# Low parts of the split weights computed on VectorE alone, in a two-block fp32 kernel on one Trainium2 core

## The chip, the cores and the metric

The program runs on one core of a Trainium2 chip. The metric is the device time of one execution in microseconds (us). One execution was also taken by the hardware profiler, and every row below comes from that one. The engines are PE (TensorE, the matrix products), DVE (VectorE), ACT (ScalarE), POOL (GpSimd) and SP (SyncE, which issues the DMAs).

## The reference

All is fp32, for 256 tokens of width 1024 (and 256 tokens of context in the first layer). A first block has two layers whose norms are scaled, shifted and gated by rows of an "ada" projection; a second block has two layers with layer norms after each step.

```python
# first block, for each of two layers
m_lat = silu(c) @ ada_w[l] + ada_b[l]           # shifts, scales, gates
h = rmsnorm(x, norm_g[l, 0]) * (1 + sc1) + sh1
y = pool_hgrn_mixer(...) if l % 2 == 0 else gqa_mixer(...)
x = x + g1 * rmsnorm(y, norm_g[l, 1])
f = swiglu(rmsnorm(x, norm_g[l, 2]) * (1 + sc2) + sh2, ffn_w_in[l], ffn_w_out[l])
x = x + g2 * rmsnorm(f, norm_g[l, 3])
...
# second block, for each of two layers
swiglu_2 = lambda x, wg, wu, wd: (silu(x @ wg) * (x @ wu)) @ wd
# x = layer_norm(alpha * x + 0.5 * swiglu_2(x))          first half step
# x = layer_norm(alpha * x + mixer(x))                   attention + RG-LRU, or delta rule
# x = layer_norm(alpha * x + 0.5 * swiglu_2(x))          second half step
# x = x + sigmoid(x @ wg + bg) * (p @ wp)                a gated embedding
```

## The kernel before

**Products.** A product of fp32 matrices is made of three products of rounded parts. A weight tile that has come by DMA (`raw`) is split by `split` (L149): ACT copies it to a rounded high part `hi` (L151), and another engine subtracts to give the low part, `lo = raw - hi` (L152). Activations are split by the same function into `xh` and `xl`, or `hh` and `hl`. `mm3` (L174, products on L176) adds hi·xh, lo·xh and hi·xl in PSUM. PSUM has tiles of four kinds, `A` (three), `B` (two), `tr` (two, for transposes) and `C` (one).

**Weights.** `piece` (L154) brings 128 x 2048 numbers of a weight by two DMAs on SP's queue (L163) into two of four `raw` tiles, and splits each in two quarters of 128 x 512: four quarters, so four ACT copies and four subtractions, for a piece. A `raw` tile is free for the next DMA when both of its quarters are split. In the second block four pieces of `hi` and `lo` are in turn.

**Where a low part is made.** `split` takes a flag: with it the subtraction goes to POOL (`self.G`), else to DVE (`self.V`). `piece` sets that flag for the second quarter of each `raw` tile when the attribute `spread` is true. `spread` is true in three places: for the first unit's weights of each feed-forward part that has one stream (`ffn`, L362; five such parts: `f1` of the first block's second layer, and `f00`, `f02`, `f10`, `f12` of the second block), through `ab2_mixer` (the second block's first mixer), and through `delta_mixer` (its second), the big projections of both among it. In all 66 subtractions go to POOL.

**Order.** Each engine works through its instructions in the order in which the build puts them. DVE's list holds the subtractions between the steps of norms and mixers; POOL's holds its subtractions between the powers (L270) that give a norm its inverse root.

**The joints between two parts.** At the end of a step of the second block `finish` in `post_ln` does, for each of the two token tiles: L1048 (add the product from PSUM), L1049 and L1053 (statistics), L275 (DVE, `rv`), L270 (POOL, `pow`), L1056 and L1058 (normalise; two halves each), then `to_xT` transposes on PE (L239, tiles `tr`) and splits. The next part's products can't start for that token tile before. In the first block the same is done by L697 (add), L662 with L270 (root), L655 (scale, tile `big`) and L239; in the gated embedding by L1094 to L1097. In `delta_mixer` a small weight `wraw` (columns 4096 to 4111) is split by `split` too, and its products (L1290) run among the first projection's; each of 24 blocks of 128 features of the projections is then evacuated by `conv`: three steps L1348 and one L1351 on DVE. In between go the 16 steps of a logarithm (L322, L324) and the products and decays of the delta rule (L1388, L1389, L1402).

**Gates.** `ada_gate` makes a gate row by a product with one column of the identity matrix; the change leaves it.

Of the kernel before, what the change touches and what calls it, by code (L numbers as in the profile page):

```python
# [9 lines left out]
F32 = mybir.dt.float32  # L10
# [3 lines left out]
ALU = mybir.AluOpType  # L14
# [67 lines left out]
class Kern:  # L82
# [40 lines left out]
    def buffers(self, es, raw, split):  # L123

        self.w = self.pool("w", 1, es, reuse_waits="tile")
        self.nraw, self.nsplit = raw, split
# [17 lines left out]
        self.tc.cur_priority -= n  # L144


    spread = False

    def split(self, hi, lo, src, pool=False):  # L149

        self.S.activation(hi, src, AF.Copy)  # L151
        (self.G if pool else self.V).tensor_tensor(lo, src, hi.bitcast(F32), op=ALU.subtract)  # L152

    def piece(self, shape, srcs, perm=None):  # L154

        hi = self.t(self.w, shape, "hi", F32R, bufs=self.nsplit)
        lo = self.t(self.w, shape, "lo", F32R, bufs=self.nsplit)
        m = shape[1] // 2
        n = shape[-1] // 2
        for h in range(2):  # L160
            raw = self.t(self.w, [shape[0], m, *shape[2:]], "raw", bufs=2 * self.nraw)
            for dst, src in srcs(raw):
                self.dma(dst, src[:, h * m:(h + 1) * m])  # L163
            for i in range(2):
                if m % 2:
                    a, b = (slice(None), h, slice(i * n, i * n + n)), (slice(None), 0, slice(i * n, i * n + n))
                else:
                    a, b = (slice(None), slice((2 * h + i) * m // 2, (2 * h + i + 1) * m // 2)), (slice(None), slice(i * m // 2, (i + 1) * m // 2))
                self.split(hi[a], lo[a], raw[b], i == 1 and self.spread)
        return hi, lo  # L170

    aside = iter(())
# [167 lines left out]
    def ffn(self, xT, streams, gate, up, down, splits, hpool, finish, ypool=None, each=None):  # L340

        gv, uv = (w.rearrange("(k p) f -> p k f", p=P) for w in (gate, up))
        dv = down.rearrange("(k p) f -> p k f", p=P)
        nS = len(streams)
        tiles = [2 * s + j for s in streams for j in range(2)]
        acc = {}
        u0 = 0
        for r, nu in enumerate(splits):  # L350
            hs, first = [], []
            for u in range(nu):
                c0 = (u0 + u) * 256
                h = [self.t(hpool, [P, nS, 2, 256], n, F32R, bufs=max(splits) + (len(splits) > 1)) for n in ("hh", "hl")]
                hs.append(h)
                if nS == 2:
                    pcs = [self.piece([P, 4, 2, 256], lambda t, k=k: [
                        (t[:, :, 0], gv[:, 4 * k:4 * k + 4, c0:c0 + 256]),
                        (t[:, :, 1], uv[:, 4 * k:4 * k + 4, c0:c0 + 256])]) for k in range(2)]
                    self.up_both(pcs, h, hpool, r == u == 0, each)  # L360
                    continue
                self.spread = u < 1  # L362
                pcs = [self.piece([P, 8, 256], lambda t, wv=wv: [(t, wv[:, :, c0:c0 + 256])]) for wv in (gv, uv)]
                self.spread = False

                if u < 2:
                    first.append((pcs, h))
                    if u:
                        for tl in tiles:
                            for pcs, h in first:  # L370
                                self.up_tile(xT[0], tl, pcs, h, hpool)
                else:
                    self.up_one(xT[0], pcs, h, hpool)
            nk = 2 * nu
            last = r == len(splits) - 1

            def hT(tl, kc):
                c = slice((tl % 2) * P, (tl % 2) * P + P)
                return [x[:, streams.index(tl // 2), kc % 2, c] for x in hs[kc // 2]]

            def out(tl, half, ps, r=r, last=last):
                if len(splits) == 1:
                    return finish(tl, half, ps, None)
                if r == 0:
                    acc[tl, half] = self.t(ypool, [P, 512], f"y{tl}_{half}")
                    self.S.activation(acc[tl, half], ps, AF.Copy)
                else:
                    self.V.tensor_add(acc[tl, half], acc[tl, half], ps)
                if last:
                    finish(tl, half, None, acc[tl, half])  # L390

            self.down(hT, tiles[2:] + tiles[:2] if last else tiles, dv[:, 2 * u0:2 * u0 + nk], nk, out)
            u0 += nu
# [730 lines left out]
    def ab2_mixer(self, xT):  # L1124
        d, V, S, G, T = self.d, self.V, self.S, self.G, self.T
        w = d["ab_w_in_2"][0]
        with self.scope("a2") as hp:
            cw, cb, ba, bx_, rate, nrate = self.rg
            gate_w = []
            for nm in ("b_wa_2", "b_wx_2"):  # L1130
                m = self.t(hp, [P, 4, P], nm)
                G.memset(m, 0.0)
                src = d[nm][0].rearrange("(b two) i j -> two i b j", two=2)
# [29 lines left out]
            kT = self.t(hp, [P, 2, 256], "kT")  # L1163
            vv = {}

            self.spread = True
            def queries(t, ps):
                q = self.t(hp, [P, 512], "q")
                S.activation(q, ps, AF.Copy)
                pt = self.pst((P, 4, P))  # L1170
                self.transposes(pt, q, range(4))
                S.activation(qT[:, :, t * P:(t + 1) * P], pt, AF.Copy)
# [63 lines left out]
            a = self.t(hp, [P, 4, 256], "a")  # L1236
# [22 lines left out]
                V.tensor_tensor_scan(hs[:, b], a[:, b], ig[:, b], 0.0, ALU.mult, ALU.add)  # L1259
            V.scalar_tensor_tensor(hs, hs, 0.5, g2, op0=ALU.mult, op1=ALU.mult)  # L1260
            self.split(cat[0][:, 4:8], cat[1][:, 4:8], hs)
            self.spread = False
        return cat


    def delta_mixer(self, xT):
        d, V, S, G, T = self.d, self.V, self.S, self.G, self.T
        w = d["c_w_in_2"][0]
        with self.scope("dl") as hp:
# [7 lines left out]
            raw = self.t(hp, [P, 8, 16], "wraw")  # L1277
# [7 lines left out]
            def rates():  # L1285

                ps = self.ps((P, 256))
                for kc in range(8):
                    for i, (x, y) in enumerate(((0, 0), (1, 0), (0, 1))):
                        T.matmul(ps, wb[x][:, kc], xT[y][:, kc], start=kc + i == 0, stop=kc == 7 and i == 2)  # L1290
                        yield
                ba = self.t(hp, [16, 256], "ba")
                S.activation(ba, ps[0:16], AF.Copy)
                pt = self.pst((P, 2, 16))
                for t in range(2):
                    T.transpose(pt[:, t], ba[:, own[t]], self.ident[0:16, 0:16])
                    yield
                S.activation(beta, pt[:, :, 0:8], AF.Sigmoid)
                V.tensor_add(ad, pt[:, :, 8:16], dtb.unsqueeze(1).to_broadcast([P, 2, 8]))
                sp = self.softplus(both(ad), 16)  # L1300
                V.scalar_tensor_tensor(g, sp.rearrange("p (t h) -> p t h", t=2), -1.0, nea.unsqueeze(1).to_broadcast([P, 2, 8]),
                                       op0=ALU.mult, op1=ALU.mult)
# [251 lines left out]
                    self.split(oT[0][:, hs, own[t]], oT[1][:, hs, own[t]], pt)  # L1554

            all4 = [(hg, t) for hg in range(2) for t in range(2)]
            self.spread = True
            with self.among(rates()):
                gates(0)
            steps = lambda *its: (x for it in its for x in it)  # L1560
# [13 lines left out]
            inverse(all4)  # L1574
            for t in range(2):
                outputs(t, range(2))
            self.spread = False
        return oT


# [4 lines left out]
    def block1(self):  # L1585
# [3 lines left out]
        with contextlib.ExitStack() as es:  # L1589
# [30 lines left out]
            def products(g):  # L1620
                for h in range(2):
                    for k in (2 * g, 2 * g + 1):
                        self.mm3(q0[h], *(x[:, k, h * P:(h + 1) * P] for x in piece), self.xh[:, :, k], self.xl[:, :, k], k == 0, k == 7)
# [210 lines left out]
```

## Time and profile before

| | |
|---|---|
| device time, 3 runs | 2187.03 us median (2185.43 to 2190.0) |
| profiled execution | 2189.62 us, of which span 2187.8 us |
| granted TensorE clock, mean of the profiled execution | 0.989 of full speed |
| PE / DVE / ACT / POOL busy | 96% / 63% / 44% / 12% of the span |

How to read the rows further down: a row of a group has the line, the engine, the operation, what it writes and reads, the number of instructions, their busy time, and the mean time of one in ns; then the idle time before them and its releaser. A row of waits says which engine and line waited for which, how long in total, how many times, and the longest. A row of the windows has, for a stretch of the span, the busy time of each engine and the granted TensorE clock.

### The profile page before, as it was taken

What the parts mean: (1) busy time and instruction counts of PE and PEld (TensorE: products, weight loads), DVE (VectorE), ACT (ScalarE), POOL (GpSimd) and SP (SyncE); (2) the same over time, 40 slices, a digit from 0 to 9 for tenths busy, and PEclk for the clock granted to TensorE, in tenths of its full rate; (3) what the DMA queues carried; (4) which work ended last, traced back from release to release, by engine and by line L of the source; (5) the groups of instructions that cost most, each with busy time, mean ns of one, the idle gap of its engine ahead of it and who ended that gap; (6) DMA issues with size and microseconds to landing.
All of it is one profiled execution on the core that took longest, in us unless ns stands there. A gap on an engine that the chain in (4) does not pass through costs nothing. (4 is left out here: it accounts for less than half of the span.)

```text
span 2187.8 us, 34008 instructions
## 1 busy us (share of the span) xinstructions
PE 2103.7 (96%) x13178; PEld 1827.5 (84%) x13178; DVE 1368.1 (63%) x2430; ACT 970.0 (44%) x1904; POOL 255.0 (12%) x248
## 2 busy tenths in 40 slices
PE   7999999999999999999999889999999999999998
PEld 4787878788887668998998778998899788879987
DVE  4746658765536786555654677555755587876556
ACT  4332353322225456444544475444544355355443
POOL 0524210000000210001000401000100155120000
PEclk9999999999999999999999999999999999999999
DMA  9632427666431334565765527655665463136653
GB/s 310 231 101 78 135 75 232 222 220 203 126 115 49 132 97 153 177 190 156 220 189 184 169 79 216 187 183 167 204 185 183 153 162 111 49 120 208 184 183 105
DMA packets 238941, 352.58 MB, mean 161 GB/s; under 512 B 14432, under 2 KB 185020, under 8 KB 238652
## 3 DMA queue, kind: packets, MB, share of 16 engines
q1 hardware_dynamic: 238780, 350.41, 51.4%
q8 instruction: 104, 1.70, 0.3%
q14 instruction: 57, 0.47, 0.1%
HBM read 349.31 MB, written 1.05 MB: 160 GB/s over the span
## 5 line engine op out<-in xcount | busy, mean ns | idle before, releaser
L151 ACT ACTIVATE hi<-raw 128x512 fp32r<-128x512 f32 (+1 forms) x1072 | 601.4, 617 | 736.3 <-issue 367.8
L152 DVE TENSOR_TENSOR lo<-raw,hi 128x512 fp32r<-128x512 f32 x1006 | 670.7, 709 | 396.0 <-ACT hi L151 394.4
L176 PE MATMUL B<-xh,hi 128*128 128x256 f32 (+1 forms) x1200 | 366.6, 306 | 1.6 <-ACT r L1141 1.4
L176 PE MATMUL B<-xl,hi 128*128 128x256 f32 (+1 forms) x1200 | 366.0, 305 | 1.0 <-DVE xl L152 0.9
L176 PE MATMUL B<-xh,lo 128*128 128x256 f32 (+1 forms) x1200 | 366.0, 305 | 0.0
L176 PE MATMUL A<-xh,hi 128*128 128x256 f32 (+1 forms) x1008 | 304.5, 302 | 3.1 <-ACT a L1389 2.9
L176 PE MATMUL A<-xh,lo 128*128 128x256 f32 (+1 forms) x1008 | 303.2, 301 | 0.7 <-DVE lo L152 0.7
L176 PE MATMUL A<-xl,hi 128*128 128x256 f32 (+1 forms) x1008 | 303.3, 301 | 0.0
L176 PEld LDWEIGHTS B<-xh,hi 128*128 128x128 f32 x1200 | 229.2, 191 | 11.9 <-ACT r L1141 1.6
L176 PEld LDWEIGHTS B<-xl,hi 128*128 128x128 f32 x1200 | 229.3, 191 | 11.2 <-DVE xl L152 1.9
L176 PEld LDWEIGHTS B<-xh,lo 128*128 128x128 f32 x1200 | 229.1, 191 | 10.1 <-issue 1.2
L176 PEld LDWEIGHTS A<-xh,hi 128*128 128x128 f32 x1008 | 193.4, 192 | 11.7 <-ACT a L1389 3.1
L176 PEld LDWEIGHTS A<-xh,lo 128*128 128x128 f32 x1008 | 193.2, 192 | 7.9 <-DVE lo L152 1.5
L176 PEld LDWEIGHTS A<-xl,hi 128*128 128x128 f32 x1008 | 193.5, 192 | 6.1
L176 PE MATMUL B<-hi,xh 128*128 128x512 f32 (+1 forms) x464 | 171.4, 370 | 5.5 <-DVE r L1048 2.7
L176 PE MATMUL B<-lo,xh 128*128 128x512 f32 (+1 forms) x464 | 169.6, 366 | 0.0
L176 PE MATMUL B<-hi,xl 128*128 128x512 f32 (+1 forms) x464 | 169.0, 365 | 0.0
L270 POOL TENSOR_TENSOR pow<-rv,mhalf 128x1 f32<-128x1 f32 (+2 forms) x54 | 43.2, 801 | 994.8 <-DVE rv L275 509.2
L152 POOL TENSOR_TENSOR lo<-raw,hi 128x512 fp32r<-128x512 f32 x66 | 96.1, 1470 | 467.0 <-ACT hi L151 464.7
L176 PE MATMUL B<-hi,hl 128*128 128x512 f32 x308 | 122.1, 396 | 0.0
L176 PE MATMUL A<-hi,hl 128*128 128x512 f32 x308 | 121.9, 396 | 0.0
L176 PE MATMUL A<-hi,hh 128*128 128x512 f32 x308 | 121.8, 395 | 0.0
(439 smaller groups left out, 3429.1 us busy)
## 6 DMA issues: line engine op xcount, KB each, us to landing
adaw<-in_ada_w SPq DMA_DIRECT2D x96, 512.0 KB, 4.8
raw<-in_ffn_wg SPq DMA_DIRECT2D x88, 512.0 KB, 4.8
raw<-in_ffn_wu SPq DMA_DIRECT2D x88, 512.0 KB, 4.6
raw<-in_ffn_wd SPq DMA_DIRECT2D x88, 512.0 KB, 4.3
raw<-in_ffn_w_in SPq DMA_DIRECT2D x88, 256.0 KB, 4.4
raw<-in_ffn_w_in SPq DMA_DIRECT2D x44, 512.0 KB, 4.4
raw<-in_ab_w_in SPq DMA_DIRECT2D x38, 512.0 KB, 4.4
raw<-in_ffn_w_out SPq DMA_DIRECT2D x38, 512.0 KB, 4.3
```

The source lines that it names most:

```text
L151: self.S.activation(hi, src, AF.Copy)
L152: (self.G if pool else self.V).tensor_tensor(lo, src, hi.bitcast(F32), op=ALU.subtract)
L176: self.T.matmul(ps, l, r, start=first and i == 0, stop=last and i == 2)
L270: self.G.tensor_tensor(r, x, exponent_tile[:, :x.shape[1]], op=ALU.pow)
```

## The change

All 66 low parts that POOL made are made by DVE. `spread` and the flag of `split` go; nothing is computed differently. The rest of POOL's work (powers, elementwise steps of the mixers, memsets) stays on POOL.

```diff
-    spread = False
-
-    def split(self, hi, lo, src, pool=False):
+    def split(self, hi, lo, src):
 
         self.S.activation(hi, src, AF.Copy)
-        (self.G if pool else self.V).tensor_tensor(lo, src, hi.bitcast(F32), op=ALU.subtract)
+        self.V.tensor_tensor(lo, src, hi.bitcast(F32), op=ALU.subtract)
...
-                self.split(hi[a], lo[a], raw[b], i == 1 and self.spread)
+                self.split(hi[a], lo[a], raw[b])
...
-                self.spread = u < 1
                 pcs = [self.piece([P, 8, 256], lambda t, wv=wv: [(t, wv[:, :, c0:c0 + 256])]) for wv in (gv, uv)]
-                self.spread = False
...
-            self.spread = True
             def queries(t, ps):
...
-            self.spread = False
         return cat
...
-            self.spread = True
             with self.among(rates()):
...
-            self.spread = False
         return oT
```

The lines of the changed kernel are a few lower (L152 is L150, L1048 is L1044, L1058 is L1054, L1348 is L1342). The order on the engines moves too, since it is made anew. Three places on DVE follow; each row is one or two instructions (x2), with the tiles' own numbers.

First, where `f00`'s last norm meets `ab2_mixer`: `lo_11037`, `lo_11051` and `lo_11369` are weights of the mixer, `r_1499` is the second token tile. Before:

```order
L152 TENSOR_TENSOR lo_11051<-raw_11052,hi_11050 128x512
L152 TENSOR_TENSOR lo_11051<-raw_11058,hi_11050 128x512
L1048 SCALAR_TENSOR_TENSOR r_1499_9030<-B_10674,r_1499_9030 128x512
L1048 SCALAR_TENSOR_TENSOR r_1499_9030<-B_10675,r_1499_9030 128x512
L1049 BN_STATS bns_10969<-r_1499_9030 128x6 x2
L152 TENSOR_TENSOR lo_11369<-raw_11370,hi_11368 128x512
L1053 BN_AGGR bna_10974<-bns_10969 128x2
L152 TENSOR_TENSOR lo_11369<-raw_11376,hi_11368 128x512
L275 TENSOR_SCALAR rv_10976<-bna_10974 128x1
L1056 SCALAR_TENSOR_TENSOR r_1499_9030<-r_1499_9030,bna_10974,lng_9025 128x512 x2
L1058 SCALAR_TENSOR_TENSOR r_1499_9030<-r_1499_9030,pow_10978,lnb_9027 128x512 x2
```

And now:

```order
L150 TENSOR_TENSOR lo_11037<-raw_11044,hi_11036 128x512 x2
L1044 SCALAR_TENSOR_TENSOR r_1499_9030<-B_10674,r_1499_9030 128x512
L1044 SCALAR_TENSOR_TENSOR r_1499_9030<-B_10675,r_1499_9030 128x512
L1045 BN_STATS bns_10969<-r_1499_9030 128x6 x2
L150 TENSOR_TENSOR lo_11051<-raw_11052,hi_11050 128x512
L1049 BN_AGGR bna_10974<-bns_10969 128x2
L150 TENSOR_TENSOR lo_11051<-raw_11052,hi_11050 128x512
L273 TENSOR_SCALAR rv_10976<-bna_10974 128x1
L1052 SCALAR_TENSOR_TENSOR r_1499_9030<-r_1499_9030,bna_10974,lng_9025 128x512 x2
L1054 SCALAR_TENSOR_TENSOR r_1499_9030<-r_1499_9030,pow_10978,lnb_9027 128x512 x2
```

The two subtractions just ahead of the second tile's norm belong to one piece now, and stand where those of two pieces stood: as many subtractions are queued ahead of L1058, and the weights that come later are pushed behind it.

Second, the same joint between `ab2_mixer`'s output product and `f02`: `lo_12008`, `lo_12022` and `lo_12038` are `f02`'s weights. Before:

```order
L1049 BN_STATS bns_11964<-r_1841_11776 128x6 x2
L152 TENSOR_TENSOR lo_12022<-raw_12029,hi_12021 128x512
L1053 BN_AGGR bna_11969<-bns_11964 128x2
L152 TENSOR_TENSOR lo_12038<-raw_12039,hi_12037 128x512
L275 TENSOR_SCALAR rv_11971<-bna_11969 128x1
L1056 SCALAR_TENSOR_TENSOR r_1841_11776<-r_1841_11776,bna_11969,lng_11771 128x512 x2
L1058 SCALAR_TENSOR_TENSOR r_1841_11776<-r_1841_11776,pow_11973,lnb_11773 128x512 x2
L152 TENSOR_TENSOR lo_12038<-raw_12039,hi_12037 128x512
L152 TENSOR_TENSOR lo_12038<-raw_12045,hi_12037 128x512
L152 TENSOR_TENSOR xl_68<-tr_11979,xh_67 128x4x128
```

And now:

```order
L1045 BN_STATS bns_11964<-r_1841_11776 128x6 x2
L150 TENSOR_TENSOR lo_12008<-raw_12015,hi_12007 128x512
L1049 BN_AGGR bna_11969<-bns_11964 128x2
L150 TENSOR_TENSOR lo_12022<-raw_12023,hi_12021 128x512
L273 TENSOR_SCALAR rv_11971<-bna_11969 128x1
L1052 SCALAR_TENSOR_TENSOR r_1841_11776<-r_1841_11776,bna_11969,lng_11771 128x512 x2
L1054 SCALAR_TENSOR_TENSOR r_1841_11776<-r_1841_11776,pow_11973,lnb_11773 128x512 x2
L150 TENSOR_TENSOR lo_12022<-raw_12023,hi_12021 128x512
L150 TENSOR_TENSOR lo_12022<-raw_12029,hi_12021 128x512
L150 TENSOR_TENSOR xl_68<-tr_11979,xh_67 128x4x128
```

Here the weights are one piece later than they were: `lo_12022`, whose split was done before the transposes, is now split around them. On PE the transposes into `tr_11979` and `tr_11986` stand 15 and 16 rows earlier than before.

Third, the projections of `delta_mixer`, in the middle of the values' blocks (`v`). Before:

```order
L1348 SCALAR_TENSOR_TENSOR cy_17136<-B_17059,colsC_9012,cy_17136 128x255
L1351 SCALAR_TENSOR_TENSOR v_2473_17044<-v_2473_17044,cy_17136 128x256
L152 TENSOR_TENSOR lo_17473<-raw_17474,hi_17472 128x512
L1348 SCALAR_TENSOR_TENSOR cy_17182<-A_17143,colsC_9012,cy_17182 128x253
L1348 SCALAR_TENSOR_TENSOR cy_17182<-A_17143,colsC_9012,cy_17182 128x254
L152 TENSOR_TENSOR lo_17473<-raw_17480,hi_17472 128x512
L1348 SCALAR_TENSOR_TENSOR cy_17182<-A_17143,colsC_9012,cy_17182 128x255
```

And now:

```order
L1342 SCALAR_TENSOR_TENSOR cy_17136<-B_17059,colsC_9012,cy_17136 128x255
L150 TENSOR_TENSOR lo_17393<-raw_17400,hi_17392 128x512
L1345 SCALAR_TENSOR_TENSOR v_2473_17044<-v_2473_17044,cy_17136 128x256
L1496 TENSOR_TENSOR b2e_2570_17630<-b_2454_16890,egc_16175 128x4
L150 TENSOR_TENSOR lo_17473<-raw_17474,hi_17472 128x512
L1342 SCALAR_TENSOR_TENSOR cy_17182<-A_17143,colsC_9012,cy_17182 128x253
L150 TENSOR_TENSOR lo_17473<-raw_17474,hi_17472 128x512
L1342 SCALAR_TENSOR_TENSOR cy_17182<-A_17143,colsC_9012,cy_17182 128x254
L150 TENSOR_TENSOR lo_17473<-raw_17480,hi_17472 128x512
```

Twice as many subtractions stand between the steps that evacuate the blocks.

## Rows read from the trace of the kernel before

**Rows 1.** The page's busy times of the engines.

```profile
PE 2103.7 (96%) x13178; PEld 1827.5 (84%) x13178; DVE 1368.1 (63%) x2430; ACT 970.0 (44%) x1904; POOL 255.0 (12%) x248
```

**Rows 2.** Instructions of L152: count, then shortest/median/longest in ns.

```profile
L152 DVE TENSOR_TENSOR lo<-raw,hi x1006: 415/685/1812, 30.9 to 2169.3; 128x512 fp32r<-128x512 f32 x164, 128x256 fp32r<-128x256 f32 x4
...
L152 POOL TENSOR_TENSOR lo<-raw,hi x66: 1264/1356/1777, 812.2 to 1959.8; 128x512 fp32r<-128x512 f32 x66
```

**Rows 3.** Groups on DVE from 900 to 1000 us, without POOL subtractions.

```profile
L152 DVE TENSOR_TENSOR lo<-raw,hi 128x512 fp32r<-128x512 f32 x70 | 44.9, 687 | 35.2 <-ACT hi L151 35.2
```

**Rows 4.** Groups on DVE from 1215 to 1233 us, the start of `ab2_mixer`.

```profile
L152 DVE TENSOR_TENSOR lo<-raw,hi 128x512 fp32r<-128x512 f32 x6 | 7.5, 1279 | 0.0
L1058 DVE SCALAR_TENSOR_TENSOR r<-r,pow,lnb 128x512 f32<-128x512 f32 x4 | 3.8, 1001 | 0.0
```

**Rows 5.** Groups on POOL from 1215 to 1233 us.

```profile
L152 POOL TENSOR_TENSOR lo<-raw,hi 128x512 fp32r<-128x512 f32 x6 | 8.7, 1463 | 3.6 <-ACT hi L151 3.5
```

**Rows 6.** Timeline of DVE there: start us, duration us (of all of a row).

```profile
1224.35 1.28 DVE L1048 SCALAR_TENSOR_TENSOR r<-B,r 128x512 f32<-128x512 f32 x2
1225.55 1.27 DVE L1049 BATCH_NORM_STATS2 bns<-r 128x6 f32<-128x512 f32 x2
...
1230.43 1.40 DVE L1058 SCALAR_TENSOR_TENSOR r<-r,pow,lnb 128x512 f32<-128x512 f32 x2
```

**Rows 7.** Waits of PE from 1215 to 1236 us.

```profile
PE tr L239 <- DVE r L1058: 3.9, 2, 3.2
```

**Rows 8.** Windows: length; busy PE, PEld, DVE, ACT, POOL; clock; DMA share; GB/s.

```profile
1768.00:1870.00 102.00, 93.58 (x722) 89.52 (x721) 81.96 (x169) 55.70 (x117) 53.37 (x42) 0.97 0.46 126
1215.00:1236.00 21.00, 17.05 (x85) 14.48 (x84) 18.22 (x24) 9.82 (x18) 11.30 (x11) 0.92 0.63 199
1536.00:1558.00 22.00, 18.94 (x102) 16.45 (x101) 19.28 (x25) 14.68 (x26) 6.42 (x4) 0.92 0.76 235
1738.00:1768.00 30.00, 25.03 (x113) 19.38 (x112) 24.39 (x30) 14.08 (x28) 16.80 (x13) 0.89 0.56 155
1948.00:1970.00 22.00, 19.52 (x93) 16.12 (x93) 18.95 (x27) 13.36 (x24) 7.23 (x5) 0.92 0.60 180
```

**Rows 9.** Waits of SP's queue over the whole span.

```profile
SPq L163 <- POOL lo L152: 70.4, 43, 4.8
```

**Rows 10.** Waits of PE from 812 to 1035 us (`f1`, and where `f00` starts).

```profile
PE tr L239 <- DVE big L655: 2.8, 2, 2.2
PE tr L239 <- DVE r L697: 2.3, 2, 1.8
```

**Rows 11.** Instructions of L655: count, then shortest/median/longest in ns.

```profile
L655 DVE TENSOR_SCALAR big<-r,pow x14: 476/486/1480, 8.0 to 843.4; 128x512 f32<-128x512 f32 x14
```

**Rows 12.** Waits of PE from 1236 to 1345 us (`ab2_mixer`, start of `f02`).

```profile
PE A L1201 <- DVE sc L1203: 1.6, 1, 1.6
PE tr L239 <- DVE r L1058: 1.5, 1, 1.5
```

**Rows 13.** Waits of PE from 1545 to 1553 us (start of `f10`).

```profile
PE A L176 <- DVE xl L152: 1.8, 1, 1.8
PE tr L239 <- DVE r L1097: 1.2, 1, 1.2
```

**Rows 14.** Waits of PE from 1738 to 1768 us (start of `delta_mixer`).

```profile
PE B L176 <- DVE r L1048: 2.7, 1, 2.7
PE A L1290 <- DVE lo L152: 1.4, 1, 1.4
PE tr L239 <- DVE r L1058: 0.8, 1, 0.8
```

**Rows 15.** Waits of PE from 1948 to 1966 us (start of `f12`).

```profile
PE tr L239 <- DVE r L1058: 2.5, 2, 1.7
```

**Rows 16.** Groups on DVE from 1768 to 1870 us, the projections of `delta_mixer`.

```profile
L152 DVE TENSOR_TENSOR lo<-raw,hi 128x512 fp32r<-128x512 f32 x24 | 21.9, 910 | 4.2 <-ACT hi L151 3.9
```

**Rows 17.** Groups on POOL from 1768 to 1870 us.

```profile
L152 POOL TENSOR_TENSOR lo<-raw,hi 128x512 fp32r<-128x512 f32 x24 | 34.2, 1438 | 24.2 <-ACT hi L151 22.3 <-issue 1.8
```

## The prediction

> **What bounds the kernel now.** I read the busy times first: PE is busy 2103.7 of 2187.8 us and DVE 1368.1 [rows 1], so the time is PE's work plus about 84 us in which PE has none, and a faster or slower DVE counts only where PE waits for it. Then the subtractions themselves: on POOL the 66 take 1.36 us in the median, on DVE 0.685 [rows 2]. Third, DVE in a stretch where POOL has none of them, and in one where it has six: 0.687 us a subtraction against 1.279, and L1058, the last step of a norm, 1.001 against 0.70 for each of the undisturbed pair that ran 1.40 [rows 3 to 6]. So work given to POOL is not free: while POOL subtracts, DVE's own instructions are lengthened, the longest subtraction to 1.812 us [rows 2]. Fourth, the waits of PE at the joints between parts, which are just where `spread` is on: each ends with a DVE instruction of the chain that the next transposes need, never with a POOL subtraction [rows 7, 10, 12 to 15]. Last the granted clock by stretch: 0.92, 0.92, 0.89 and 0.92 at four of these joints [rows 8]; the low stretches follow the waits, so a wait costs twice.
>
> So the question is at each joint: does DVE finish the awaited step sooner if it makes the subtractions itself, and is no longer lengthened by POOL?
>
> **What the change adds on DVE.** 66 instructions. One takes 0.685 us, but the next starts sooner than that: two L1048 begin at 1224.35 and the instruction after them at 1225.55, 0.60 us each [rows 6]. 66 x 0.60 = 39.6 us. What it gives back I price from the same stretches: from 1215 to 1233 us it is 6 x (1.279 - 0.687) = 3.6 on subtractions and 4 x (1.001 - 0.70) = 1.2 on L1058, 4.8 together, against six POOL subtractions [rows 3 to 6], which are 6 x 0.60 = 3.6 of added work. In `delta_mixer`'s projections it is 24 x (0.910 - 0.687) = 5.4 on the subtractions alone, against 24 x 0.60 = 14.4 added [rows 3, 16, 17]. In sum DVE's work hardly shrinks; what moves is which instruction is late. At a joint the lengthened ones are those that PE waits for, and the order shows no more subtractions ahead of L1058 than before (the later weights stand behind it), so there the lengthening is gained and the added work falls after the transposes, beside products.
>
> The Trainium skill speaks for this in "SBUF — State Buffer", Who interferes with whom: a DVE instruction with two SBUF inputs contends with a GpSimd instruction that reads SBUF, and the one that comes second waits for the whole of the first. By that rule a subtraction or an L1058 behind a POOL subtraction costs up to POOL's whole duration more, and all of it comes back; the rows agree in size, 1.812 - 0.685 = 1.13 us at most, under POOL's shortest 1.264 [rows 2].
>
> **Joint by joint.** Each term is the wait of the trace less what the shorter chain leaves.
> 1. `f1`'s start: L655 took up to 1.480 us where its median is 0.486 [rows 11], and PE waited 2.2 for it at once [rows 10]. Gain 1.0 there, 0.5 on small steps before it: -1.5.
> 2. `f00`'s start: the longest wait for L697 is 1.8 [rows 10]; two lengthened instructions ahead of it (up to 1.13 each) give all but 0.1 back: -1.7.
> 3. `ab2_mixer`'s start: PE waits 3.9 for L1058, 3.2 of it at the second token tile [rows 7]. Ahead stand six subtractions and the first L1058 pair, 4.8 us lengthened as above, and as many subtractions ahead as before: the wait shrinks to 0.3, -3.6. With it the low clock: (1 - 0.92) x 21 = 1.7 [rows 8]. Together -5.3.
> 4. Inside `ab2_mixer`: 1.6 for L1203 [rows 12]. Subtractions queued ahead of it still wait for ACT, so I take -0.5.
> 5. `f02`'s start: 1.5 for L1058 [rows 12] goes, but the transposes stand 15 rows earlier on PE and two more subtractions lie between them and the splits, so a wait of the same size is likely in another place: 0, between -1.5 and +1.5.
> 6. `f10`'s start: 1.8 and 1.2 [rows 13]; the gated embedding's steps are lengthened too. All but 0.5 of it: -2.5. Clock (1 - 0.92) x 22 = 1.8 [rows 8]. Together -4.3.
> 7. `delta_mixer`'s start: the 2.7 and 0.8 [rows 14] fall to 1.4, -2.1; the 1.4 for `wraw`'s low part [rows 14], which stood behind subtractions lengthened to about 1.2, to 0.2: -1.2. Clock (1 - 0.89) x 30 = 3.3 [rows 8]. Together -6.6.
> 8. `delta_mixer`'s projections: DVE is busy 82.0 of 102 us [rows 8], and gets 14.4 more. Given back are 5.4 on subtractions by the rows, and more on L1351 and the small steps of the logarithm between them, which no row here prices singly. Ends: all 14.4 given back and PE's waits there unchanged (0), and 14.4 - 5.4 = 9.0 all on the path. DVE would hold 82.0 + 9.0 = 91.0 of 102, so it still fits, but evacuations come later and two `B` and three `A` tiles give little slack. I take +2, near the lower end, since 20 us of idle time can absorb most of it.
> 9. `f12`'s start: 2.5 for L1058 [rows 15], of which a lengthened pair is the larger part: -2.0. Clock (1 - 0.92) x 22 = 1.8 [rows 8]: -3.8.
>
> Sum: -1.5 - 1.7 - 5.3 - 0.5 + 0 - 4.3 - 6.6 + 2 - 3.8 = -21.7 us, of which the clock is 8.6. The clock comes back only if the remaining gaps are short enough, so I take -20. Of the profiled execution's 2189.6 that leaves 2169.6; this execution lies 2.6 above the median of the runs, and I set the same -20 against the median: 2187.0 - 20 = **2167 us**. The cover for the added work at the joints is PE's products of the first weights; if that cover is gone (weights late for their first product), each subtraction ahead of one is 0.60 on the path. SP's queue, which waited 70.4 us in 43 places for POOL to free a `raw` tile [rows 9], gains up to 0.7 us at each (1.36 against 0.685); since no joint's wait ends with a DMA I count nothing for it, and the few small constants and norm vectors that change places in it are needed much later. POOL's own chain (`pow` between L275 and L1058) loses its neighbours, no cost.
>
> **Rivals.**
> (a) DVE becomes the bound in the projections and the gain is taken back. For it: 82.0 of 102 us busy before, and 24 subtractions more. The lower parts that PE needs next stand in one list with the evacuations that free its PSUM tiles. Price: 14.4 - 5.4 = 9.0 on the path, and the joints' gain without the clock (-21.7 - 2 + 8.6 = -15.1): -6, 2181. It decides the sign only if nothing is given back at all: 14.4 exposed here, and at the joints 42 subtractions at 0.60 = 25 of which perhaps half lie ahead of an awaited step, 14.4 + 12.6 - 15 = +12, **2199**; the point is where DVE's work for two feature blocks passes PE's time for them. Against it: the rows show the lengthening [rows 2 to 4], so something must come back.
> The skill has this as a rule: "Perfetto Trace Analysis", Optimizing Scalar/DVE Operations, says that where DVE is saturated it may make sense to hand work to another engine, even GPSIMD, with the warning that a shared read port may eat it. DVE is busy 18.22 of 21 us at one joint [rows 8], so the rule would keep the work on POOL; its warning is what the lengthened rows show.
> (b) The gains don't last: PE starts a part earlier and then waits for the weights, since ACT's high parts and the DMAs keep their pace, and the clock falls elsewhere. Then joints 3, 6, 7 and 9 keep a quarter of their sum of 20.0, and the rest stands: 5 + 3.7 - 2 = -6.7; with term 8 at 9.0 it is 0: **2181 to 2187**.
> (c) The change doesn't do what it says: the long DVE rows are not POOL's doing but wait for operands or for PSUM, and stay. Against it: L655 and L1058 read SBUF only, and their long rows lie in stretches with `spread` on. Then DVE has only more to do: the slow end of (a), 2199.
>
> **How the numbers follow.** A measurement here can tell 0.2%, 4.4 us. The forecast (gains at the joints, 2160 to 2178 by its own bounds: term 8 between 0 and 9, clock back or not in part) has 0.68; the weak cases of (a) and (b), 2178 to 2187, 0.22, of which 0.12 lies faster than 2182.6 and 0.10 within 0.2%; the slow end of (a) with (c) 0.10, of which 0.01 lies within it. Faster by over 0.2%: 0.68 + 0.12 = 0.80; within: 0.10 + 0.01 = 0.11; slower: 0.09. The range leaves out about 0.1 below, where more waits vanish than I counted, and 0.1 above: 2157 to 2186.
>
> **What would show it.** Right: no DVE subtraction above 0.75 us in the whole trace, L1058 and L655 at their medians everywhere; the waits of 3.2 at 1228 us and of 2.7 at 1745 us below 0.5 and about 1.4; granted clock 1.00 at the four joints; DVE about 10 us busier or not at all. Wrong: long DVE rows that stay (then (c)); PE waits for `cy` or `lo` in the projections that sum to over 5 us (then (a)); waits of PE for `hi` or for weights some us after each joint (then (b)). The forecast is most exposed to term 8 and to the clock, together 12 of its 20 us.

## The result: 1.4% faster, and half as much again as forecast

The changed kernel takes 2157.45 us in the median of four runs (2153.12 to 2161.91), the kernel before 2188.52 in the runs beside it; the ratio is 0.9861, with an interval of 0.984 to 0.9883. A second set of runs gave 0.9849 (0.983 to 0.9869). The forecast was 2167 us, a gain of 20; measured are 31, on the side forecast and just inside the range, whose lower end is 2157. The profiled execution has a span of 2156.3 us.

The page's row of the engines, which answers to [rows 1]:

```profile
PE 2093.5 (97%) x13178; PEld 1819.7 (84%) x13178; DVE 1365.8 (63%) x2496; ACT 970.5 (45%) x1904; POOL 160.0 (7%) x182
```

POOL has lost 95 us of work and DVE has 66 instructions more, yet DVE is busy 2.3 us less than before. At 0.60 us each the 66 are 39.6 us, so by this estimate about 42 us came back from instructions that are no longer lengthened: the balance of the forecast ("DVE's work hardly shrinks"), on the whole span. One by one, instructions of three lines, with their count and the shortest/median/longest in ns (L150 makes the low parts, L1054 is the last step of a norm, L651 is L655 before):

```profile
L150 DVE TENSOR_TENSOR lo<-raw,hi x1072: 416/685/1786, 30.4 to 2138.0; 128x512 fp32r<-128x512 f32 x175, 128x256 fp32r<-128x256 f32 x4
...
L1054 DVE SCALAR_TENSOR_TENSOR r<-r,pow,lnb x24: 743/746/751, 1214.6 to 2132.5; 128x512 f32<-128x512 f32 x24
...
L651 DVE TENSOR_SCALAR big<-r,pow x14: 476/486/488, 8.2 to 844.0; 128x512 f32<-128x512 f32 x14
```

L651 took up to 1.480 us before [rows 11], and L1058 had a mean of 1.001 at one joint [rows 4]; now no instance is longer than 0.488 and 0.751. A few subtractions are still long, up to 1.786 us: POOL keeps other work with two operands.

The granted clock and busy times at the same joints, which answer to [rows 8] (length; PE, PEld, DVE, ACT, POOL; clock; DMA share; GB/s). The stretches are earlier by what has been gained until there:

```profile
1208.00:1229.00 21.00, 21.00 (x110) 17.62 (x110) 18.55 (x33) 9.80 (x18) 2.85 (x5) 1.00 0.43 121
1527.00:1549.00 22.00, 21.20 (x134) 18.93 (x134) 18.79 (x32) 16.65 (x28) 0.00 (x0) 1.00 0.79 243
1725.00:1751.00 26.00, 25.11 (x139) 20.37 (x138) 23.29 (x40) 16.11 (x30) 3.70 (x3) 1.00 0.68 184
1920.00:1942.00 22.00, 22.00 (x126) 19.07 (x125) 19.85 (x36) 12.22 (x22) 1.85 (x2) 1.00 0.56 167
1748.00:1842.00 94.00, 92.61 (x721) 89.36 (x720) 83.60 (x196) 57.57 (x120) 23.26 (x19) 0.96 0.50 141
```

At the first four the clock is full where it was 0.92, 0.92, 0.89 and 0.92, and at two of them PE has no idle time at all. The last row, the projections of `delta_mixer`, is the surprise: they fit into 94 us where they took 102, at the same clock (0.96 and 0.97), and DVE is busy 83.6 us there against 82.0, with the 24 subtractions more that POOL made before.

What is left of the waits of PE, at `f1` and the start of `f00`, and at the start of `delta_mixer`, to be held against [rows 10] and [rows 14]:

```profile
PE tr L237 <- DVE big L651: 2.0, 2, 1.2
PE tr L237 <- DVE r L693: 1.0, 2, 0.6
...
PE tr L237 <- DVE r L1054: 0.6, 1, 0.6
PE B L174 <- DVE r L1044: 0.2, 1, 0.2
```

The longest waits there are 1.2 and 0.6, where they were 2.2 and 1.8; the 2.7 has become 0.2, and the 1.4 for `wraw` is gone, as are all waits at the starts of `ab2_mixer` and `f12`.

### The profile page after: what moved, and what is told of

Same layout as the page of the kernel before. It is cut to its first block, busy times and chain, and to the rows that moved or that the text cites. A ratio compares the mean times of both kernels' runs of the same rounds, so it can differ in the third digit from the quotient of the medians.

```text
span 2156.3 us, 33891 instructions
## 1 busy us (share of the span) xinstructions
PE 2093.5 (97%) x13178; PEld 1819.7 (84%) x13178; DVE 1365.8 (63%) x2496; ACT 970.5 (45%) x1904; POOL 160.0 (7%) x182
## 5 line engine op out<-in xcount | busy, mean ns | idle before, releaser
L150 DVE TENSOR_TENSOR lo<-raw,hi 128x512 fp32r<-128x512 f32 (+1 forms) x1072 | 696.3, 692 | 381.2 <-ACT hi L149 379.8
L174 PE MATMUL A<-lo,hh 128*128 128x512 f32 x308 | 121.9, 396 | 0.1
```

The source lines that it names most:

```text
L150: self.V.tensor_tensor(lo, src, hi.bitcast(F32), op=ALU.subtract)
L174: self.T.matmul(ps, l, r, start=first and i == 0, stop=last and i == 2)
```

## Where the time went, stage by stage

To place a gain I took, from each trace, the start of the PE instruction of the same rank (median of 17 neighbours) and subtracted its start in the trace of before. The change of that difference over a stage is what the stage gave (minus) or cost (plus), in us. The stages are given by their times in the trace of before. The other columns are the experiments of the next section.

```
stage (us of before)          after  dup_pool set_pool dup_dve delta_only ffn_only ab2_only delta_joint delta_proj
f1 start         760-850      -0.9    +3.4     -1.2    -1.3    -0.8       +0.2     -0.8     -0.6        -0.8
f00 start       1018-1035     -1.4    +0.7     -1.5    -1.4    -1.4        0.0     -1.4     -1.4        -1.4
ab2 start       1210-1236     -5.9    -4.3     -5.5    -5.4    -5.9       -5.9     +1.0     -5.8        -5.8
inside ab2      1250-1256     -1.6    -0.9     -2.3    -1.5    -1.6       -1.6     +0.8     -1.5        -1.5
before f02      1300-1315     -2.8    -1.2     +2.1    -1.1    -1.2       -1.4     -1.4     -1.2        -2.8
f02 start       1326-1345     +1.4    +2.7     +1.0    +2.1    +2.0        0.0     +1.8     +1.6        +2.2
f10 start       1530-1558     -3.9    +0.6     -4.0    -4.1    -4.1       -0.2     -4.0     -3.8        -3.9
delta start     1730-1768     -7.3    -4.2     -7.4    -6.9    -1.2       -7.3     -7.3     -3.0        -5.3
projections     1768-1870     -8.0    +6.6     -5.3    -2.3    +0.8       -5.9     -6.0     -9.4        +2.1
f12 start       1948-1966     -4.1    -3.2     -4.1    -4.2    -4.2       +0.2     -4.1     -4.1        -4.1
```

The stages between are within 2.5 us, but for the first 760 us, in which executions differ by up to 7.3 us however alike the kernels are there, and 4.0 between 1870 and 1940 in `dup_pool`. The column of the change sums to -34.5; the stages between and the first 760 us take back 3.1, which leaves the 31.4 by which its last products are earlier.

How far such a number can be trusted, a second trace of the changed kernel shows (`after_again`, below). It has the same numbers within 0.3, but for -4.7 at `f10` and -10.3 in the projections. The projections differ by the granted clock. The first trace's row is 1748.00:1842.00 above; the second's, with the same columns, is:

```profile
1746.00:1839.00 93.00, 90.74 (x726) 86.98 (x724) 84.19 (x198) 58.33 (x120) 23.63 (x19) 1.00 0.51 144
```

In the traces that have these low parts on DVE and nothing added there, the projections gave 9.4 to 11.5 where the clock was 1.00, 8.0 where it was 0.96 and 5.9 to 6.0 where it was 0.95. At the start of `f1` kernels that are alike there lie between -1.8 and +1.2.

## The experiments

**The same DVE work, with POOL reading, POOL writing, or DVE doing it twice.** Three kernels compute all low parts on DVE, as the changed kernel does. At the 66 places they add something that nobody needs, in the raw tile whose last reader has been, each with one of the three last lines:

```diff
-        (self.G if pool else self.V).tensor_tensor(lo, src, hi.bitcast(F32), op=ALU.subtract)
+        self.V.tensor_tensor(lo, src, hi.bitcast(F32), op=ALU.subtract)
+        if pool:
+            self.G.tensor_tensor(src, src, hi.bitcast(F32), op=ALU.subtract)   # dup_pool
+            self.G.memset(src, 0.0)                                            # set_pool, three times
+            self.V.tensor_tensor(src, src, hi.bitcast(F32), op=ALU.subtract)   # dup_dve
```

> All 66 low parts are made by DVE as in the changed kernel; POOL then repeats each of the 66 subtractions with the result in the used-up raw tile (nobody reads it; the raw tile is held until then). Theory (POOL's two-operand reads lengthen DVE's instructions, and that is what the joints and the projections paid): the waits of 2 to 3 us at the joints come back, all 31 us of the gain and some for DVE's own added work, 2185 to 2205 us, with DVE subtractions of up to 1.8 us. Rival (POOL was late as the maker of low parts, or its place in the order did it, not its reads): 2157 to 2163 us, no wait at a joint above 1.5 us.

> As dup_pool, but POOL fills the used-up raw quarter three times with zeros (about 0.53 us each, 1.6 us together) instead of subtracting: it holds the raw tile as long and is as busy, but reads nothing. Theory (its reads contend): 2157 to 2163 us, DVE subtractions at 0.685 us. Rival (the raw tile is held longer and the DMAs come late, or any POOL work does it): as slow as dup_pool, 2175 us or more.

> As dup_pool, but DVE itself repeats the 66 subtractions into the raw tile: 66 x 0.60 = 39.6 us of work more on DVE, none on POOL. Theory (DVE has room; what cost time was an awaited instruction lengthened by POOL, not DVE's sum of work): 2160 to 2172 us. Rival (DVE is the bound around the joints and in the projections, so its sum of work sets the time): 39.6 us mostly exposed, 2180 to 2197 us.

Measured, against the kernel before: `dup_pool` 1.002 (1.0005 to 1.0035), 2197.2 us; `set_pool` 0.988 (0.9857 to 0.9902), 2164.3; `dup_dve` 0.9902 (0.9879 to 0.9925), 2169.6. The pages' rows of the engines, in that order:

```profile
PE 2107.7 (96%) x13178; PEld 1829.7 (83%) x13178; DVE 1405.6 (64%) x2496; ACT 971.0 (44%) x1904; POOL 253.9 (12%) x248
```

```profile
PE 2094.1 (97%) x13178; PEld 1819.8 (84%) x13178; DVE 1364.8 (63%) x2496; ACT 973.1 (45%) x1906; POOL 262.9 (12%) x380
```

```profile
PE 2095.7 (97%) x13178; PEld 1818.5 (84%) x13178; DVE 1403.0 (65%) x2562; ACT 973.3 (45%) x1906; POOL 160.5 (7%) x182
```

This settles what lengthens DVE. 66 subtractions on POOL, about 94 us of them, add 39.8 us of busy time to a DVE with the same 2496 instructions (1405.6 against 1365.8); 198 fills on POOL, 103 us of them, add none in sum (1364.8). It is POOL's reading. It is what the Trainium skill says in "SBUF — State Buffer", Who interferes with whom: a DVE instruction with two SBUF inputs contends with a GpSimd instruction that reads SBUF, not with one that only writes. In the projections of the two kernels (group: count, busy us, mean ns), `dup_pool` first:

```profile
L152 DVE TENSOR_TENSOR lo<-raw,hi 128x512 fp32r<-128x512 f32 x51 | 48.5, 958 | 0.1
```

```profile
L152 DVE TENSOR_TENSOR lo<-raw,hi 128x512 fp32r<-128x512 f32 x49 | 37.4, 766 | 1.2 <-ACT hi L151 1.1
```

And it settles that DVE's sum of work alone is not the price. `dup_dve` and `dup_pool` load DVE equally (1403.0 and 1405.6 us), and lie 28 us apart. In `dup_dve` the added 37 us cost 9 to 12 (by the ratios, 0.9902 against 0.9861, or by the times, 2169.6 against 2157.5): two thirds of it or more is hidden beside PE's products. A lengthened instruction stands anywhere in the list, ahead of an awaited one too. Most of what `dup_dve` does pay, it pays in the projections, 5.7 us by the table. There DVE is busy 92.4 of 100 us and PE waits for it 7.4, over the 5 us that the prediction had named as the sign of rival (a); so there the room on DVE is used up by some 9 us of work more than the changed kernel's:

```profile
PE B L178 <- DVE lo L152: 3.5, 6, 1.1
PE A L1404 <- DVE cy L1350: 3.3, 3, 1.5
```

The joints of `dup_pool` met the expectation in part only. Its waits of 2 to 3 us came back at `f00` (2.7), `f10` (2.6 and 1.0) and the start of `delta_mixer` (2.2 and 1.4); at the starts of `ab2_mixer` and `f12` single waits are 1.4 and 0.9, where the kernel before had 3.2 and 1.7. Its POOL subtractions stand elsewhere than in the kernel before, each behind DVE's own. At the start of `ab2_mixer` one of them (1.74 us, from 1232.61) lengthens a pair of the norm's steps, which takes 1.40 undisturbed:

```profile
1232.45 2.44 DVE L1058 SCALAR_TENSOR_TENSOR r<-r,bna,lng 128x512 f32<-128x512 f32 x2
```

`set_pool` was expected within 6 us of the changed kernel and is 7 above it by the times, 4 by the ratios. By the table of stages, 4.9 lie before `f02`, a matter of the clock (below), and 2.7 in the projections, where PE waits again for the decays' exponentials on ACT:

```profile
PE A L179 <- ACT a L1392: 3.1, 1, 3.1
PE A L1405 <- ACT a L1392: 1.9, 1, 1.9
```

The fills hold the raw tiles for another 1.6 us and more when they queue up; in this trace ACT's high parts just ahead of those exponentials wait for the DMA into such a tile (2.9 and 2.4 us). So holding raw tiles costs something too, about 3 us here; it isn't what most of the time went into. In the kernel before itself ACT waits for no DMA in the projections, so there this cost did not arise. `dup_pool` holds the tiles too (ACT waits 17.7 us for DMAs in the projections, 9.2 in the changed kernel). It stands 14.6 us above the changed kernel there: PE waits 12.0 us against 1.9, and it is busy 97.9 at a clock of 0.91 against 92.6 at 0.96. I can't part reading and holding in its waits.

**One part at a time.** Five kernels keep POOL's low parts in one part and have all else on DVE, by leaving `self.spread = True` in one of its places (for `delta_joint` until after `gates(0)`, for `delta_proj` from there on).

> POOL keeps its low parts in delta_mixer alone; the feed-forward parts and ab2_mixer have theirs on DVE. From the two traces the delta part gained 7.3 us at its start and 8.0 in its projections, less 0.8 later. Theory (the parts add up, each by its own joint): 2157.5 + 14.5 = 2172 us. Rival (the gain in the projections was a chance of order or of the clock, as I forecast +2 there): 2157.5 + 7 = 2164 us or less.

> POOL keeps its low parts in the five feed-forward parts alone (20 subtractions). From the two traces the changed kernel is ahead by 0.9 at the start of f1, 1.4 at f00, -2.3 at f02, 3.9 at f10 and 4.1 at f12, 8.0 together. Theory (each joint's gain belongs to its own subtractions): 2157.5 + 8.0 = 2165.5 us. Rival (neighbouring parts share the gain, since a joint has subtractions of the part before and after it): off by more than 4 us.

> POOL keeps its low parts in ab2_mixer alone. From the two traces: 5.9 us at its start, 1.6 inside, and 2.8 of a clock window after a wait that is the same in both. Theory: 2157.5 + 7.5 = 2165 us, and the 2.8 are a chance of the clock; with them 2168 us. Rival (the joint's gain is an earlier start that is given back): under 2161 us.

> POOL keeps its low parts in delta_mixer's first projection alone (the z gates at its start), all else on DVE. Theory: the start's 7.3 us come back, 2157.5 + 7.3 = 2165 us, with the waits of 2.7 and 1.4 us there. Rival: the gain at the start needs the later subtractions too (under 2161 us).

> POOL keeps its low parts in delta_mixer after its first projection, all else on DVE. Theory (POOL's reads make L1348 and L1351 late, ACT's list behind them late, and PE waits 3 us twice for the decays' exponentials): 2157.5 + 8 = 2165 us, with PE waits for ACT L1389 of 2 us or more. Rival (my forecast: DVE has more to do without POOL, so POOL helps here): 2153 to 2157 us.

Measured ratios to the kernel before: `delta_only` 0.9925 (0.9902 to 0.9947), `ffn_only` 0.9903 (0.9883 to 0.9923), `ab2_only` 0.9913 (0.988 to 0.9946), `delta_joint` 0.9868 (0.9852 to 0.9885), `delta_proj` 0.9923 (0.9899 to 0.9947). Times 2188.5 us these are 2172, 2167, 2169, 2160 and 2172; expected were 2172, 2165.5, 2165 to 2168, 2165 and 2165. The kernels ran beside executions of before that were 3 to 4 us slower, so ratios are compared here, not times.

The table of stages is sharper than the ratios. At the joints each part's gains vanish in the kernel that keeps that part on POOL, and in none of the other four: `ffn_only` alone loses those at `f00`, `f10` and `f12`, `ab2_only` alone those of `ab2_mixer`, and the kernels with POOL in `delta_mixer` those there. (In the projections `ffn_only` and `ab2_only` are 2 us short of the changed kernel, at a clock of 0.95.) At two joints the waits come back to the tenth. At the start of `ab2_mixer` in `ab2_only`, and at the start of `f12` in `ffn_only`, [rows 7] and [rows 15] again:

```profile
PE tr L239 <- DVE r L1057: 3.9, 2, 3.2
```

```profile
PE tr L239 <- DVE r L1058: 2.5, 2, 1.7
```

Within `delta_mixer` the expectation failed. The start alone (`delta_joint`) costs 4.3 us by the table, of which 1.4 comes back in the projections, and its 2160 us lie on the side of its rival (under 2161): the wait of 2.7 is there again, the 1.4 for `wraw` is not. The projections alone (`delta_proj`) cost 10.1 there and 2.0 before. In `delta_proj` PE's waits in the projections are these:

```profile
PE A L1400 <- ACT a L1387: 3.0, 1, 3.0
PE A L176 <- ACT a L1387: 2.9, 1, 2.9
PE B L176 <- DVE cy L1346: 1.9, 2, 1.2
PE A L1386 <- DVE cy L1346: 1.9, 2, 1.1
```

**The one joint that got worse, undone.** In the table `f02`'s start costs 1.0 to 2.7 us in every kernel that makes its low parts on DVE, and nothing in the one that doesn't. `f02_keep` is the changed kernel with POOL's four low parts there:

```diff
-                self.spread = u < 1
+                self.spread = u < 1 and self.keep
...
+                            self.keep = i == 0 and n == 2
```

> The changed kernel, but POOL keeps the four low parts of f02's first unit. In the traces of the kernels so far the start of f02 is 1.4 to 2.2 us later than in the kernel before wherever those four are on DVE, and level with it where they are on POOL. Theory (that start is the one joint at which the change costs time): 1.4 to 2 us faster than the changed kernel, 0.9985 to 0.999 of it. Rival (the wait is only moved to the next products): no difference.

> The changed kernel once more, beside the two that follow. Theory and rival alike: 0.986 of the kernel before (0.984 to 0.988).

2155.91 us, 0.9843 (0.9825 to 0.9862), beside 2157.05 and 0.9849 (0.983 to 0.9869) of the changed kernel in the same set. In its trace `f02`'s start costs 0.2 us where the changed kernel's, twice, cost 1.4 and 1.7. So the trace has the 1.2 to 1.5 us, and the runs can't tell the two kernels apart: it beats the kernel before, and the changed one only by the trace.

**POOL's remaining two-operand work in the projections.** `act_decays` is the changed kernel with L1380 on ACT:

```diff
-                G.tensor_tensor(dec[c], m3(after), b3(g[:, t, 4 * hg:4 * hg + 4]), op=ALU.mult)
+                for h in range(4):
+                    S.activation(dec[c][:, h], after, AF.Copy, scale=g[:, t, 4 * hg + h:4 * hg + h + 1])
```

> The changed kernel, but the four two-operand products of POOL that open the decays (line L1380, about 1.25 us each) are made by ACT, as 16 copies with a scale of one column. Theory (what is left of the long DVE instructions in the projections, 8.3 us against 20.0 before, is POOL's remaining two-operand work, and PE no longer waits for it): DVE's excess falls by about 4 us and the time by 0 to 2 us. Rival (ACT's list, which PE waited for in the kernel before, gets 4 us more and is late again): 2 to 6 us slower.

2158.32 us, 0.9853 (0.9831 to 0.9875): no difference. The mean of a subtraction in the projections fell from 772 ns to 740 and DVE's busy time there by about 2 us, half of what was expected. PE's waits there are 0.8 and 0.7 us, against 1.9 in all in the changed kernel; with so little waiting there was next to nothing to gain.

```profile
L150 DVE TENSOR_TENSOR lo<-raw,hi 128x512 fp32r<-128x512 f32 x49 | 37.7, 772 | 0.5 <-ACT hi L149 0.4
```

```profile
L150 DVE TENSOR_TENSOR lo<-raw,hi 128x512 fp32r<-128x512 f32 x51 | 37.4, 740 | 0.6 <-ACT hi L149 0.5
```

## Why the prediction was right, and where it was short

**The mechanism** held at the joints: awaited DVE instructions were lengthened by POOL's reads, and at a joint the lengthening comes back while the added work falls behind it. Rival (c) is excluded by `dup_pool` against `set_pool`. Rival (a) is excluded for this change by `dup_dve`: even 37 us more on DVE leave the kernel faster than before, though its sign appears in the projections. Rival (b) didn't come: behind each joint the difference stays, and the stages between give back 0.9 us at most. One reading was off: the pair of L1058 in [rows 6] overlaps, so 1.40 for two isn't 0.70 for each. Undisturbed, one takes 0.746 us, and the term of 1.2 in the 4.8 us was 1.0. That the time lies inside the range at all is close: it is 0.5 us above its lower end.

**Terms 1 to 7 and 9** sum to -23.7 in the forecast (its -21.7 less the +2 of the projections) and to -23.7 in the table; that the sums agree to a tenth is luck, since single terms are off by up to 1.4 and the start of `f1` varies by more than its term between kernels that are alike there. One by one, forecast and measured: `f1` -1.5 and -0.9; `f00` -1.7 and -1.4; `ab2` start -5.3 and -5.9; inside it -0.5 and -1.6; `f02` 0 and +1.4, the new wait that the order showed, inside its bounds; `f10` -4.3 and -3.9; delta start -6.6 and -7.3; `f12` -3.8 and -4.1. The clock came back at all four joints, as counted.

**Term 8 is the step that failed.** I gave the projections +2 between 0 and +9; they gave -8.0, and -5.9 to -11.5 in the other traces that have these low parts on DVE, by the granted clock. Two things were wrong. First the price of what comes back: I had 5.4 us from the rows of subtractions and said that the rest was unpriced. DVE's busy time says 82.0 + 14.4 - 83.6 = 12.8. Little of it was the term that I had priced: the mean of a subtraction stayed at 772 ns, so of the 5.4 us about 4.2 were still lost, now over 49 subtractions. Most of it was in short instructions that I had named in part and priced nowhere. In the kernel before, the same stretch:

```profile
L1371 DVE TENSOR_TENSOR b<-beta,rk 128x4 f32<-128x4 f32 x4 | 4.5, 1116 | 2.7 <-POOL rk L1370 2.7
...
L322 DVE TENSOR_TENSOR lpacc<-lpacc,lpz 128x16 f32<-128x16 f32 x8 | 3.3, 407 | 0.0
L324 DVE TENSOR_SCALAR lpacc<-lpacc 128x16 f32<-128x16 f32 x8 | 3.2, 399 | 0.0
```

and in the changed one:

```profile
L1365 DVE TENSOR_TENSOR b<-beta,rk 128x4 f32<-128x4 f32 x4 | 1.5, 366 | 1.2 <-POOL rk L1364 1.2
...
L320 DVE TENSOR_TENSOR lpacc<-lpacc,lpz 128x16 f32<-128x16 f32 x8 | 1.3, 166 | 0.0
L322 DVE TENSOR_SCALAR lpacc<-lpacc 128x16 f32<-128x16 f32 x8 | 1.3, 166 | 0.0
```

These three groups give back 6.9 us. The 12.8 alone would have made the balance about +1.6, still no gain. The second error was the lower end of 0, "PE's waits there unchanged". PE waited 7.7 us there in the kernel before, 5.9 of it for ACT, and I had taken an ACT wait for none of DVE's business. One step further back ACT had waited for DVE. Waits of PE, then of ACT, in the projections before:

```profile
PE A L1402 <- ACT a L1389: 3.0, 1, 3.0
PE A L176 <- ACT a L1389: 2.9, 1, 2.9
PE A L1388 <- DVE cy L1348: 1.8, 2, 1.0
```

```profile
ACT v L1350 <- DVE cy L1348: 10.4, 6, 3.9
ACT q L1350 <- DVE cy L1348: 8.8, 6, 2.7
ACT r L1350 <- DVE cy L1348: 8.2, 6, 2.2
```

ACT works through its list in order, so an exponential behind a `q` that waits for DVE is late though its own operand is there. The second wait shows it. PE's products for the last exponentials (L1388) ended at 1829.0, ACT began the exponentials (L1389) at 1831.47 and 1832.46, and the two `q` ahead of them had waited 2.69 and 1.46 us for `cy`. On PE, then on ACT (start us, us):

```profile
1827.92 1.10 PE L1388 MATMUL A<-a,c_upto 128*128 128x512 f32 x2 [0.77 <-DVE cy L1348]
```

```profile
1827.87 0.42 ACT L1350 ACTIVATE q<-cy 128x256 f32<-128x256 f32 x1 [2.69 <-DVE cy L1348]
1829.75 0.42 ACT L1350 ACTIVATE q<-cy 128x256 f32<-128x256 f32 x1 [1.46 <-DVE cy L1348]
...
1831.47 0.59 ACT L1389 ACTIVATE a<-A 128x512 f32<-128x512 f32 x1
```

DVE's timeline up to the end of the wait of 2.69 us:

```profile
1822.40 1.32 DVE L1351 SCALAR_TENSOR_TENSOR q<-q,cy 128x256 f32<-128x256 f32 x1 [0.55 <-ACT q L1350]
1823.65 0.47 DVE L1348 SCALAR_TENSOR_TENSOR cy<-A,colsC,cy 128x253 f32<-128x253 f32 x1
1824.04 1.66 DVE L152 TENSOR_TENSOR lo<-raw,hi 128x512 fp32r<-128x512 f32 x1
1825.62 0.47 DVE L1348 SCALAR_TENSOR_TENSOR cy<-A,colsC,cy 128x254 f32<-128x254 f32 x1
1826.01 1.37 DVE L152 TENSOR_TENSOR lo<-raw,hi 128x512 fp32r<-128x512 f32 x1
```

Three of these five instructions are 0.7 to 1.0 us too long, 2.6 together. In the changed kernel ACT's waits in the projections are

```profile
ACT hi L149 <- DMA raw<-in_c_w_in: 9.2, 11, 1.6
ACT v L1344 <- DVE cy L1342: 5.7, 5, 2.1
```

and PE waits 1.9 us in all; these waits are 5.8 of the 8.0 us. `delta_proj` shows that POOL's share in the projections brings both waits for ACT back, and ACT waits for no DMA there either, so a raw tile that POOL holds is not what they came from. Not shown is how much of it is the lengthening and how much the order: in ACT's list four high parts stood between the last `q` and the first of these exponentials in the kernel before, and one stands there now, and no kernel kept the one and changed the other.

**Outside the terms** lie 2.8 us before `f02`. After a wait of 3.0 us that is the same in both kernels (PE for a low part of the embedding) the clock fell in one execution and not in the other:

```profile
1294.00:1316.00 22.00, 18.48 (x66) 14.05 (x67) 16.60 (x22) 12.89 (x21) 2.42 (x1) 0.84 0.65 217
```

```profile
1285.00:1307.00 22.00, 18.09 (x76) 13.86 (x77) 16.90 (x22) 13.88 (x23) 2.42 (x1) 1.00 0.70 223
```

Of the other executions three gained 2.8 there too (the changed kernel's second trace among them), seven 1.1 to 1.4, and `set_pool` lost 2.1. I take it for a chance of these executions, not for the change, but that isn't shown.

One sign that I had named for "right" failed: no subtraction above 0.75 us. The remaining long ones, up to 1.786 us, cost no wait that is left to gain, as `act_decays` shows for the projections.

## What to carry to other kernels

An offload to GpSimd that reads two operands from SBUF can be paid for on VectorE: here 66 subtractions of 1.4 us on POOL cost DVE as much as doing them itself (about 40 us), and at unplanned places. So price such an offload by what is awaited: list the waits of the bounding engine in the stretch, follow each releaser back until it waits for nothing, and look whether a lengthened instruction is on that way, in a list in between too. And look at the shortest instructions of the busy engine there first, since here they were lengthened by the largest factor: the 128x16 steps to 2.4 times, the 128x512 subtractions of the same stretch to 1.3 times. And count the room that is left on the busy engine: with 92.4 of 100 us busy in `dup_dve`, PE did wait for it.

## What the runs showed of the hardware

- POOL's reading lengthens DVE, its writing doesn't: 66 subtractions on POOL added 39.8 us to DVE's busy time, 198 fills of the same tiles none in sum. A small exception are `tensor_scalar` steps: the 128x16 ones took 0.191 us in the mean in `set_pool`, up to 0.26 beside a fill, against 0.166 in the changed kernel.
- Instructions with one tensor operand were lengthened too: L655, a multiplication of one SBUF tile by a column, from 0.486 to 1.480 us [rows 11], 0.06 us behind the start of a POOL subtraction, and the 128x16 steps of L324 from 0.166 to 0.399 in the mean. The Trainium skill, in the section of "SBUF — State Buffer" named above, has `tensor_scalar` among the operations that can take the shared port; I had looked for two-operand instructions alone.
- The same idle time of 3.0 us on PE was followed by a granted clock of 0.84 in one execution and of 1.00 in another. A term for the clock behind a wait is a term with a chance: here it came as counted at four joints, and unasked at a fifth.
